# 35 pairs of projection blocks by seven half-size products, and the branch projections behind the mLSTM heads

## The chip, the cores and the metric
One core of a Trainium2 chip runs the kernel in one launch. The metric is device time in microseconds (us); the median of the runs is compared. The engines are PE (TensorE: matmuls, with PEld as its weight loads), DVE (VectorE), ACT (ScalarE), POOL (GpSimd) and SP (SyncE, which issues the transfers).

## The reference
One layer of a streaming encoder on 576 tokens (512 of a new stream, 64 of a running one), model width 1024:

```
h = rmsnorm(x);  p = h @ w_in                      # 1024 x 7880, columns split into 12 parts
hm = mlstm(conv(xcm), vm, i, f) * sigmoid(o)       # 4 heads of width 256, chunks of 64 tokens in the reference
ha = mla(c_q, c_kv, k_r)                           # 8 attention heads on latents
p_m = (hm * silu(z_m)) @ w_pm                      # 1024 x 1024
p_a = (ha * silu(z_a)) @ w_pa                      # 1024 x 1024
y = x + (sigmoid(g_m) * p_m + sigmoid(g_a) * p_a) @ w_out
```

States and caches of both streams are outputs too. Everything is float32.

## The kernel before
Each float32 operand is split in a high and a low part, and a product is three matmuls (hi hi, hi lo, lo hi). The inputs' parts (`hhi`, `hlo`) stay in SBUF with the features on partitions. A **block** is 128 output columns for all 576 tokens: `fblock` (L150) loads 512 KB of weights by `wload` (L107, two `raw` buffers), ACT writes the high part (128x1024, L104), DVE subtracts the low part (L105), and `gemm_f` (L120) issues 48 matmuls at L126: two halves of 288 tokens, three products, eight parts of the inner dimension, each half in its own PSUM bank (`MM`, two buffers).

There are 72 such blocks' worth of work: 8 each of z_a (Z), g_m (G) and g_a, 32 in the four mLSTM heads (conv input, o, z_m, v), 8 of w_pa and 8 of w_pm. With the heads' own q and k products that is 3,648 matmuls at L126.

The order: normalised input and latents (`START`); then the attention loop, which follows `PLAN`: K (keys and queries of a pair of heads, L567), H (a head, L524), Z (`z_block` L516), G (`gm_block` L170, its result goes to a DRAM scratch) and P (`proj_a` L584: a pair of heads times w_pa, added up in the SBUF tile `part`, L593 and L595). Then four mLSTM heads (`mhead` L685): `conv_block` (L638) x2, `gate_block` (L673) x2, `v_block` (L659) x2, q and k, and the loop over chunks (L730), where POOL makes the scaled queries (L752, split at L105) and a reciprocal root (L74). The g_a blocks (`ga_block` L614, L619) stand around the heads: one before, seven after. Then w_pm with the merge (L815 to L826), and w_out with the residual (L828 to L854). Weights are split as they arrive, on ACT and DVE, one or two blocks ahead.

A scheduler in the framework sets the order of each engine's instructions when the program is built, and it moves independent blocks between the steps of the attention and of the chunk loop. So the order that runs is the built one, not that of the text. The PSUM is split in pools of 2 banks (`pmm`), 3 (`psa`) and 3 (`psk`), L46 to L48.

Of the kernel before, what the change touches and what calls it, by code (L numbers as in the profile page):

```python
# [27 lines left out]
# order in which the work of the first two stages is issued (see `steps` and the attention loop)  # L28
START = "X0 A Q X1 C0 X2 B C1 S X3 X4 T0 L T1 T3 C3 C2 C4 T2 R T4 J"
PLAN = "G0 K0 Z0 H0 Z1 K1 H1 G2 G1 Z2 P0 H2 Z3 Z4 H3 G3 K2 P1 H4 G4 Z5 Z6 H5 G5 K3 Z7 P2 H6 H7 G6 G7 P3"  # L30
# [7 lines left out]
def layer(ctx: ExitStack, tc, A, O):  # L38
# [7 lines left out]
    pmm = mkpool(ctx, "pmm", 2, space=PSUM)  # L46
    psa = mkpool(ctx, "psa", 3, space=PSUM)
# [3 lines left out]
    wts = mkpool(ctx, "wts")  # L51
    hpool = mkpool(ctx, "hT")
    gp = mkpool(ctx, "gates")
    pp = mkpool(ctx, "part")

    def MM():
        return [pmm.tile([P, 512], F32, tag="mm", name="mm")[:, 0:HT] for _ in range(2)]
# [61 lines left out]

    def gemm_f(ps, w, x, nk, c0=0, k0=0):  # L120
        whi, wlo = w
        xhi, xlo = x
        trip = [(a, b, k) for a, b in ((whi, xhi), (whi, xlo), (wlo, xhi)) for k in range(nk)]
        for j, sl in enumerate(HALVES):
            for n, (a, b, k) in enumerate(trip):
                pe.matmul(ps[j], a[:, k0 + k, c0:c0 + P], b[:, k, sl], start=(n == 0), stop=(n == len(trip) - 1))  # L126
# [23 lines left out]
    def fblock(wd, col, x):  # L150
        w = wload([wd[:, col:col + P]], KB, P)
        ps = MM()
        gemm_f(ps, w, x, KB)
        return ps

    hx = (hhi, hlo)

# [10 lines left out]
    part = pp.tile([P, KB, T], F32, name="part")  # L168

    def gm_block(f, tg):  # L170
        z = fblock(A["w_in"], O_GM + f * P, hx)
        for j, sl in enumerate(HALVES):
            act.activation(tg[:, sl], z[j], AF.Tanh, scale=0.5)
        sp.dma_start(gmscr[f], tg)

    mla_es = ctx.enter_context(ExitStack())
    mp = mkpool(mla_es, "mla", side="right")
    cqhi = mp.tile([P, 3, T + DEC], F32R, name="cqhi")
# [3 lines left out]
    krhi = mp.tile([P, TK], F32R, name="krhi")  # L182
    krlo = mp.tile([P, TK], F32R, name="krlo")
# [4 lines left out]
    with ExitStack() as es:  # L188
        s0 = mkpool(es, "start0", side="right")
        s1 = mkpool(es, "start", side="right")  # L190
        sw = mkpool(es, "startw", side="right")
        s2 = mkpool(es, "start2", side="right")
# [13 lines left out]
        cgk = s2.tile([P, 5, ROPE], F32, name="cgk")  # L206
        sgk = s2.tile([P, 5, ROPE], F32, name="sgk")
        gq = s2.tile([P, ROPE], F32, name="gq")

        def load_small():  # L210
# [5 lines left out]
            for cg, sg, g in ((cgk, sgk, small["g_kr"]), (cgq, sgq, gq)):  # L216
# [34 lines left out]
        def x_tile(n):  # L251
            t0, L = TILES[n]
            xt = s1.tile([P, D], F32, tag="xt", name="xt", bufs=3)
# [4 lines left out]
            xs = s1.tile([P, D], F32, tag="xs", name="xs", bufs=1)  # L258
            act.activation(xs[0:L], xt[0:L], AF.Square, scale=D ** -0.5, accum_out=st[0:L, 0:1])
# [80 lines left out]
        def gates():  # L340
            # log-sigmoid, running sums and maxima; rows are (chunk, head)
# [77 lines left out]
        def load_q():  # L419
# [3 lines left out]
                 "T": ck_tile, "R": past, "J": gates,  # L423
                 "G": lambda f: gm_block(f, s1.tile([P, D], F32, tag="xt", name="tg", bufs=3)[:, 0:T])}
# [4 lines left out]
    with ExitStack() as es:  # L429
        hap = mkpool(es, "ha", side="right")  # L430
        cw = mkpool(es, "cw", side="right")
        ap = mkpool(es, "att", side="right")
        ak = mkpool(es, "atk", side="right")
        aq = mkpool(es, "atq", side="right")
# [81 lines left out]
        def z_block(h):  # L516
            z = fblock(A["w_in"], O_ZA + h * P, hx)
            za = aq.tile([P, T], F32, tag="za", name="za", bufs=2)
            for j, sl in enumerate(HALVES):
                act.activation(za[:, sl], z[j], AF.Tanh, scale=0.5)  # L520
                dve.scalar_tensor_tensor(za[:, sl], za[:, sl], 1.0, z[j], ALU.add, ALU.mult)
            return za

        def head(hh, qT, qrT, kT, v, za, ha):  # L524
# [29 lines left out]
            pTs = aq.tile([P, 2, DEC], F32, tag="pTs", name="pTs", bufs=1)  # L554
# [10 lines left out]
            split_of(ha[0][:, hh], ha[1][:, hh], za)  # L565

        def kq(p):  # L567
# [4 lines left out]
            wk = wload([A["w_ukv"][:, 512 * p:512 * (p + 1)]], 2, 512, cw, 6 * QH)  # L572
            wq = wload([A["w_uq"][:, 2 * QH * p:2 * QH * (p + 1)]], 3, 2 * QH, cw, 6 * QH)
# [10 lines left out]
        def proj_a(p, ha):  # L584
            for c in range(2):
# [38 lines left out]
    with ExitStack() as es:  # L624
# [60 lines left out]
        def mhead(h):  # L685
# [14 lines left out]
            for e in range(2):  # L700
                v_block(2 * h + e, va, e)
# [204 lines left out]
```

## Time and profile before

| | |
|---|---|
| median of 3 runs (lowest, highest) | 824.47 us (824.22, 824.84) |
| profiled execution, first to last instruction | 822.5 us |
| PE busy | 810.0 us, 98% |
| DVE busy | 478.7 us, 58% |
| ACT busy | 362.0 us, 44% |
| POOL busy | 141.4 us, 17% |
| HBM read, written | 64.24 MB, 7.61 MB |

The profiled execution has only its span, 822.5 us; the median of the runs is 2.0 us above it. Busy shares are means over stages: input and attention run up to about 368 us, the mLSTM heads and g_a to 714 us, w_pm to 765 us, and w_out to the end.

### The profile page before, as it was taken

What the parts mean: (1) busy time and instruction counts of PE and PEld (TensorE: products, weight loads), DVE (VectorE), ACT (ScalarE), POOL (GpSimd) and SP (SyncE); (2) the same over time, 40 slices, a digit from 0 to 9 for tenths busy, and PEclk for the clock granted to TensorE, in tenths of its full rate; (3) what the DMA queues carried; (4) which work ended last, traced back from release to release, by engine and by line L of the source; (5) the groups of instructions that cost most, each with busy time, mean ns of one, the idle gap of its engine ahead of it and who ended that gap; (6) DMA issues with size and microseconds to landing.
All of it is one profiled execution on the core that took longest, in us unless ns stands there. A gap on an engine that the chain in (4) does not pass through costs nothing.

```text
span 822.5 us, 14924 instructions
## 1 busy us (share of the span) xinstructions
PE 810.0 (98%) x5759; PEld 761.5 (93%) x5759; DVE 478.7 (58%) x1211; ACT 362.0 (44%) x999; POOL 141.4 (17%) x253
## 2 busy tenths in 40 slices
PE   7899999999999999999999999999999999999998
PEld 6898997888898798889999999999999999999997
DVE  5666566755576658545534873775477355655431
ACT  5446556663555654322434544444454434332200
POOL 2343241410143133001001110110111011000000
PEclk9999999999999999999999999999999999999999
DMA  8431231013113011126223232333333432543332
GB/s 267 138 108 59 74 111 27 1 52 106 41 52 120 27 41 33 46 84 157 78 77 91 66 106 74 103 84 97 91 94 96 118 87 68 165 124 106 101 95 76
DMA packets 101742, 72.80 MB, mean 89 GB/s; under 512 B 5742, under 2 KB 95848, under 8 KB 101672
## 3 DMA queue, kind: packets, MB, share of 16 engines
q1 hardware_dynamic: 101672, 71.86, 30.5%
q8 instruction: 45, 0.74, 0.4%
q14 instruction: 25, 0.20, 0.1%
HBM read 64.24 MB, written 7.61 MB: 87 GB/s over the span
## 4 chain that ended last, share of the span: by engine, by line
PE 94%; DMA 3%; DVE 1%; ACT 1%; issue 0%; SPq 0%; POOL 0%; DVEq 0%; ACTq 0%
PE mm L126 58%; PE sk L143 10%; PE sk L852 3%; PE sa L852 3%; PE sa L529 2%; PE sa L728 2%; PE sa L559 2%; PE sk L728 2%; PE sk L136 2%; PE sa L531 1%; PE sa L547 1%; PE sk L745 1%; PE sa L136 1%; PE sk L502 1%; DMA part<-in_w_in 1%; DMA E<-gscr 1%
## 5 line engine op out<-in xcount | busy, mean ns | idle before, releaser
L105 DVE TENSOR_TENSOR wlo<-raw,whi 128x1024 fp32r<-128x1024 f32 (+1 forms) x88 | 108.5, 1234 | 92.1 <-ACT whi L104 87.1
L104 ACT CAST whi<-raw 128x1024 fp32r<-128x1024 f32 (+1 forms) x88 | 92.6, 1055 | 135.2 <-PE mm L126 91.9
L126 PE MATMUL mm<-hhi,whi 128*128 128x288 f32 x896 | 147.1, 300 | 1.1 <-ACT hhi L104 1.1
L126 PE MATMUL mm<-hhi,wlo 128*128 128x288 f32 x896 | 146.6, 299 | 0.0
L126 PE MATMUL mm<-hlo,whi 128*128 128x288 f32 x896 | 145.7, 298 | 0.0
L126 PEld LDWEIGHTS mm<-hhi,whi 128*128 128x128 f32 x896 | 126.6, 188 | 2.1 <-ACT hhi L104 1.4
L126 PEld LDWEIGHTS mm<-hlo,whi 128*128 128x128 f32 x896 | 127.1, 188 | 1.3 <-issue 0.5
L126 PEld LDWEIGHTS mm<-hhi,wlo 128*128 128x128 f32 x896 | 126.9, 188 | 1.2 <-issue 0.5
L74 POOL TENSOR_TENSOR r<-r,mhalf 128x2 f32<-128x2 f32 (+3 forms) x44 | 37.2, 844 | 165.4 <-DVE r L495 109.4
L126 PE MATMUL mm<-ha,whi 128*128 128x288 f32 x256 | 48.2, 307 | 0.6 <-DVE part L595 0.6
L126 PEld LDWEIGHTS mm<-ha,whi 128*128 128x128 f32 x256 | 37.3, 188 | 2.7 <-DVE part L595 1.1
L511 ACT ACTIVATE P<-sa,sc 128x128 f32<-128x128 f32 (+4 forms) x40 | 20.1, 503 | 36.4 <-DVE sc L510 35.6
L752 POOL TENSOR_TENSOR qi<-qf,wi 128x256 f32<-128x256 f32 (+1 forms) x16 | 11.9, 744 | 105.7 <-ACT qf L710 54.3
L595 DVE TENSOR_TENSOR part<-part,mm 128x288 f32<-128x288 f32 x48 | 21.4, 452 | 11.8 <-PE mm L126 11.6
L74 POOL TENSOR_TENSOR sc<-sc,mhalf 128x1 f32<-128x1 f32 (+1 forms) x20 | 13.0, 648 | 87.0 <-DVE sc L784 87.0
L126 PE MATMUL mm<-ha,wlo 128*128 128x288 f32 x128 | 27.5, 296 | 0.0
L105 POOL TENSOR_TENSOR qi<-qi,qi 128x256 fp32r<-128x256 f32 (+1 forms) x16 | 10.7, 668 | 85.3 <-ACT qi L104 85.3
L529 PE MATMUL sa<-kT,qT 128*128 128x128 f32 (+3 forms) x64 | 23.4, 447 | 0.0
L510 DVE TENSOR_REDUCE sc<-sa 128x1 f32<-128x128 f32 (+4 forms) x40 | 18.3, 457 | 8.5 <-PE sa L532 6.4
L728 PE MATMUL sk<-va,kw 128*128 128x258 f32 (+1 forms) x120 | 22.2, 290 | 0.1
L823 DVE SCALAR_TENSOR_TENSOR mt<-tgm,mm 128x288 f32<-128x288 f32 x16 | 7.3, 454 | 25.1 <-PE mm L126 25.1
L474 ACT ACTIVATE qT<-sk,gqn_c 128x128 f32<-128x128 f32 (+1 forms) x40 | 12.2, 354 | 18.8 <-PE sk L472 18.8
(353 smaller groups left out, 1641.0 us busy)
## 6 DMA issues: line engine op xcount, KB each, us to landing
raw<-in_w_in SPq DMA_DIRECT2D x56, 512.0 KB, 3.8
raw<-in_w_pa SPq DMA_DIRECT2D x8, 512.0 KB
raw<-in_w_pm SPq DMA_DIRECT2D x8, 512.0 KB, 4.2
raw<-in_w_uq SPq DMA_DIRECT2D x4, 576.0 KB, 4.0
gmscr<-tg SPq DMA_DIRECT2D x8, 288.0 KB
tgm<-gmscr SPq DMA_DIRECT2D x8, 288.0 KB, 4.3
xt<-in_x_prompt SPq DMA_DIRECT2D x4, 512.0 KB, 6.7
raw<-in_w_ukv SPq DMA_DIRECT2D x4, 512.0 KB, 3.8
```

Of the source, the lines that this page charges most:

```text
L74: pool.tensor_tensor(dst, ms, mhalf[0:n, 0:dst.shape[-1]], op=ALU.pow)
L104: act.copy(hi, src)
L105: (eng or dve).tensor_tensor(lo, src, hi.bitcast(F32), op=ALU.subtract)
L126: pe.matmul(ps[j], a[:, k0 + k, c0:c0 + P], b[:, k, sl], start=(n == 0), stop=(n == len(trip) - 1))
L136: pe.matmul(out, x[:, k, t0:t0 + P], a, start=(i == 0), stop=(i == len(trip) - 1))
L143: pe.matmul(out, b[:, k, t0:t0 + L], a[:, k, c0:c0 + n], start=(i == 0), stop=(i == len(trip) - 1))
L510: dve.tensor_reduce(sc[0:L, 0:1], ps, AX.X, ALU.max, negate=True)
L511: act.activation(pt[0:L, 0:n], ps, AF.Exp, bias=sc[0:L, 0:1], accum_out=sc[0:L, 1:2])
L529: pe.matmul(ps[:, 0:n], qT[hh][:, q0:q0 + P], kT[hh][:, 0:n], start=True, stop=False)
L595: dve.tensor_tensor(part[:, f, sl], part[:, f, sl], ps[j], op=ALU.add)
L728: pe.matmul(out, x, y, start=(first and i == 0), stop=(last and i == 2))
L852: pe.matmul(ps[0:L, 0:NB], x[:, 4 * u + k, t0:t0 + L], w[u][i][:, k], start=(q == 0), stop=(q == len(trip) - 1))
```

## The change
Two neighbouring blocks with the two halves of the inner dimension and the two halves of the tokens form a 2x2 by 2x2 product of half-size matrices. `spair` computes it by seven products (Strassen in Winograd's form) instead of eight: 7 x 12 matmuls of 288 columns (three split products, four parts of the inner dimension) instead of 96. The seven weight matrices are four sub-blocks of `raw` and three sums, with a fourth sum for the last product; POOL makes four sums in place in `raw`, and each of the seven is split on its own. The inputs' sums T1 to T4 are made once per operand. The results are put together partly in a PSUM bank that several products add to, with ACT copies (three) and DVE adds (three) between.

35 pairs go this way: Z 4, g_m 3, heads 16, g_a 4, w_pa 4, w_pm 4. One g_m pair stays plain (`G0`). The program has 5,210 matmuls instead of 5,630. `ha`, `hm` and the gates of g_a go to DRAM scratch; w_pa is no longer part of the attention loop, it stands behind the heads, and the sums for `ha` and `hm` are made there (`operand`).

```diff
-PLAN = "G0 K0 Z0 H0 Z1 K1 H1 G2 G1 Z2 P0 H2 Z3 Z4 H3 G3 K2 P1 H4 G4 Z5 Z6 H5 G5 K3 Z7 P2 H6 H7 G6 G7 P3"
+PLAN = "K0 Z0 H0 K1 H1 Z1 M1 H2 H3 K2 Z2 M2 H4 H5 K3 Z3 M3 H6 H7"
+N_SA = 3
+RING = 5
-    pmm = mkpool(ctx, "pmm", 2, space=PSUM)
+    pst = mkpool(ctx, "pst", space=PSUM)
-    psk = mkpool(ctx, "psk", 3, space=PSUM)
+    psk = mkpool(ctx, "psk", 5 - N_SA, space=PSUM)
+    def combos(f11, f12, f21, f22, dst, eng):
+        eng.tensor_tensor(f11, f12, f11, op=ALU.subtract)
+        split_of(*dst[0], f11)
+        eng.tensor_tensor(f12, f22, f12, op=ALU.subtract)
+        eng.tensor_tensor(f22, f22, f11, op=ALU.subtract)
+        split_of(*dst[1], f22)
+        split_of(*dst[2], f12)
+        eng.tensor_tensor(f21, f21, f22, op=ALU.subtract)
+        split_of(*dst[3], f21)
+    def spair(wd, col, X, ct):
+        raw = rawp.tile([P, 2 * D], F32, tag="raw", name="raw", bufs=2).rearrange("p (k c) -> p k c", k=KB)
+        sp.dma_start(raw, wd[:, col:col + 2 * P].rearrange("(k p) c -> p k c", p=P))
+        f11, f12, f21, f22 = (raw[:, k:k + KH, c:c + P] for c in (0, P) for k in (0, KH))
...
+        a11 = sw(f11)
+        pool.tensor_tensor(f11, f11, f21, op=ALU.subtract)
+        pool.tensor_tensor(f21, f21, f22, op=ALU.add)
+        px, pz = bank(tx), bank(tz)
+        prod(px, a11, "B11", True)
+        act.copy(ct[:, 0, 0:HT], px)
+        s1 = sw(f21)
+        pool.tensor_tensor(f21, f22, f11, op=ALU.subtract)
+        prod(pz, s1, "T1", True)
+        act.copy(ct[:, 1, HT:T], pz)
+        s2 = sw(f21)
+        prod(px, s2, "T2", False)
+        act.copy(ct[:, 0, HT:T], px)
+        a12 = sw(f12)
+        pool.tensor_tensor(f12, f12, f21, op=ALU.subtract)
+        py = bank(ty)
+        prod(py, a12, "B21", True)
+        dve.tensor_tensor(ct[:, 0, 0:HT], ct[:, 0, 0:HT], py, op=ALU.add)
+        s3 = sw(f11, 1)
+        prod(px, s3, "T3", False)
+        dve.tensor_tensor(ct[:, 1, HT:T], ct[:, 1, HT:T], px, op=ALU.add)
+        s4 = sw(f12, 1)
+        prod(pz, s4, "B22", False)
+        dve.tensor_tensor(ct[:, 0, HT:T], ct[:, 0, HT:T], pz, op=ALU.add)
+        a22 = sw(f22, 1)
+        prod(px, a22, "T4", False)
+        return px
+    def gated(lp, tag, ct, scr, wd, q, p):
+        tg = lp.tile([P, 2, T], F32, tag=tag, name="tg", bufs=2)
+        sp.dma_start(tg, scr[2 * p:2 * p + 2].rearrange("f p t -> p f t"))
+        px = spair(wd, 2 * p * P, q, ct)
+        dve.scalar_tensor_tensor(tg[:, 0], tg[:, 0], 1.0, ct[:, 0], ALU.add, ALU.mult)
+        dve.scalar_tensor_tensor(tg[:, 1, HT:T], tg[:, 1, HT:T], 1.0, ct[:, 1, HT:T], ALU.add, ALU.mult)
+        dve.scalar_tensor_tensor(tg[:, 1, 0:HT], tg[:, 1, 0:HT], 1.0, px, ALU.add, ALU.mult)
+        return tg
...
         for h in range(H_M):
-            if h == 0:
-                ga_block(0, lp)
             mhead(h)
-        for f in range(1, KB):
-            ga_block(f, lp)
+        for p in range(KB // 2):
+            gate_out(PT(), O_GA, gascr, p)
...
+        operand(f1, "g", hascr, aq)
+        for p in range(KB // 2):
+            ct = PT()
+            ta = gated(lp, "gm", ct, gascr, A["w_pa"], aq, p)
+            sp.dma_start(gascr[2 * p:2 * p + 2].rearrange("f p t -> p f t"), ta)
+        operand(f1, "g", hmscr, hq)
...
+            tg = gated(lp, "gm", ct, gmscr, A["w_pm"], hq, p)
+            dve.tensor_tensor(tg, tg, ta, op=ALU.add)
+            split_of(mt[0][p], mt[1][p], tg)
```

`sw` gives a sub-block's high and low part a slot in a ring of five (`wh`, `wl`), from the heads on with three further slots for the last three of a pair; `operand` loads a branch's result from scratch and makes its 14 split parts, with `combos` on POOL (8 sums of 128x576).

On PE, in the w_pm stage, one block was three rows of 16 matmuls in two groups; the names are output bank, input part and weight part.

```order
L126 MATMUL mm<-hmhi,whi 128x288 x8
L126 MATMUL mm<-hmlo,whi 128x288 x8
L126 MATMUL mm<-hmhi,wlo 128x288 x8
L126 MATMUL mm<-hmhi,whi 128x288 x8
L126 MATMUL mm<-hmlo,whi 128x288 x8
L126 MATMUL mm<-hmhi,wlo 128x288 x8
```

Now, in the same stage, the products of two pairs stand between each other (banks b_9595 and b_9596 are of one pair, b_9735 and b_9736 of the next).

```order
L205 MATMUL b_9595<-hhi,wh_9664 128x288 x4
L205 MATMUL b_9595<-hlo,wh_9664 128x288 x4
L205 MATMUL b_9595<-hhi,wl_9665 128x288 x4
L205 MATMUL b_9735<-hhi,wh 128x288 x4
L205 MATMUL b_9735<-hlo,wh 128x288 x4
L205 MATMUL b_9735<-hhi,wl 128x288 x4
L205 MATMUL b_9736<-T1h,wh 128x288 x4
L205 MATMUL b_9736<-T1l,wh 128x288 x4
L205 MATMUL b_9736<-T1h,wl 128x288 x4
L205 MATMUL b_9595<-T4h,wh_9698 128x288 x4
L205 MATMUL b_9595<-T4l,wh_9698 128x288 x4
L205 MATMUL b_9595<-T4h,wl_9699 128x288 x4
```

So two products of the next pair (24 matmuls) stand between the last two products of a pair that add to one bank.

On POOL, in the chunk loop of a head, there were a scaled query, its split and a reciprocal root per chunk (`qi`, `sc`).

```order
L105 TENSOR_TENSOR qi_7323<-qi,qi_7322 128x256
L752 TENSOR_TENSOR qi<-qf,wi 128x256
L74 TENSOR_TENSOR sc<-sc,mhalf 128x1
L105 TENSOR_TENSOR qi_8236<-qi,qi_8235 128x256
L752 TENSOR_TENSOR qi<-qf,wi 128x256
L74 TENSOR_TENSOR sc<-sc,mhalf 128x1
```

Now the sums of the weights in `raw` stand between them (head 3, with g_a pairs beside it).

```order
L870 TENSOR_TENSOR qi<-qf,wi 128x256
L221 TENSOR_TENSOR raw<-raw 128x4x128
L208 TENSOR_TENSOR raw<-raw 128x4x128
L209 TENSOR_TENSOR raw<-raw 128x4x128
L214 TENSOR_TENSOR raw<-raw 128x4x128
L75 TENSOR_TENSOR sc<-sc,mhalf 128x1
L221 TENSOR_TENSOR raw<-raw 128x4x128
L106 TENSOR_TENSOR qi_8006<-qi,qi_8005 128x256
```

The root of a chunk stands behind up to four sums of 128x512.

On DVE, at the start of w_pm, each block had one split of 128x1024, two merges out of PSUM, an add and a split of the merged block.

```order
L823 SCALAR_TENSOR_TENSOR mt<-tgm,mm 128x288
L105 TENSOR_TENSOR hlo<-mt,hhi 128x576
L823 SCALAR_TENSOR_TENSOR mt<-tgm,mm 128x288
L105 TENSOR_TENSOR wlo<-raw,whi 128x1024
L824 TENSOR_TENSOR mt<-mt,part 128x576
```

Now, behind the heads, the splits of `ha` and its sums (`aB11l` to `aT4l`, from the tile `g`) stand in a row with weight splits and an add (L227).

```order
L106 TENSOR_TENSOR wl_8803<-raw,wh_8802 128x512
L227 TENSOR_TENSOR ct<-ct,b_8516 128x288
L106 TENSOR_TENSOR aB21l<-g,aB21h 128x576
L106 TENSOR_TENSOR aB22l<-g,aB22h 128x576
L106 TENSOR_TENSOR aT1l<-g,aT1h 128x576
L106 TENSOR_TENSOR aT3l<-g,aT3h 128x576
L106 TENSOR_TENSOR wl_8820<-raw,wh_8819 128x512
L106 TENSOR_TENSOR wl_8837<-raw,wh_8836 128x512
L106 TENSOR_TENSOR aT2l<-g,aT2h 128x576
L106 TENSOR_TENSOR aT4l<-g,aT4h 128x576
L106 TENSOR_TENSOR aB11l<-g,aB11h 128x576
```

Weight splits that PE needs next stand in the same queue as the splits of the operand.

## Rows read from the trace of the kernel before
**Rows 1.** The page, busy time of each engine (us, share of the span, instructions).

```profile
PE 810.0 (98%) x5759; PEld 761.5 (93%) x5759; DVE 478.7 (58%) x1211; ACT 362.0 (44%) x999; POOL 141.4 (17%) x253
```

**Rows 2.** Engine waits on PE, the two largest (total us, times, longest).

```profile
PE sa L267 <- DVE xs L262: 2.7, 2, 1.4
PE sk L203 <- DVE wrm L200: 1.5, 1, 1.5
```

**Rows 3.** Windows: length; PE, PEld, DVE, ACT, POOL busy; clock, DMA share, GB/s.

```profile
0.00:368.00 368.00, 359.99 (x2304) 317.78 (x2305) 231.27 (x665) 192.85 (x650) 97.12 (x181) 1.00 0.26 77
368.00:714.00 346.00, 345.44 (x2624) 339.45 (x2623) 203.68 (x477) 150.46 (x326) 39.96 (x56) 1.00 0.34 94
714.00:765.30 51.30, 51.30 (x389) 51.28 (x388) 26.02 (x38) 13.91 (x19) 3.31 (x14) 1.00 0.44 130
765.30:822.50 57.20, 53.22 (x449) 53.01 (x447) 17.71 (x32) 4.75 (x6) 1.03 (x2) 0.99 0.29 88
558.20:630.50 72.30, 72.30 (x553) 70.93 (x553) 45.45 (x113) 33.43 (x75) 9.88 (x14) 1.00 0.35 96
```

**Rows 4.** Chain of waits, the w_pm piece (start us, us, what).

```profile
714.33 50.97 PE mm L126 x384
```

**Rows 5.** Groups by shape, whole span (count | busy us, mean ns | idle before).

```profile
L105 DVE TENSOR_TENSOR ulo<-acc,uhi 128x512 fp32r<-128x512 f32 x8 | 5.5, 684 | 0.7 <-ACT uhi L104 0.7
L105 DVE TENSOR_TENSOR ha<-za,ha 128x576 fp32r<-128x576 f32 x8 | 6.1, 768 | 2.5 <-ACT ha L104 2.5
L105 DVE TENSOR_TENSOR hmlo<-tm,hmhi 128x1152 fp32r<-128x1152 f32 x4 | 5.4, 1356 | 1.7 <-ACT hmhi L104 1.7
L595 DVE TENSOR_TENSOR part<-part,mm 128x288 f32<-128x288 f32 x48 | 21.4, 452 | 11.8 <-PE mm L126 11.6
L104 ACT CAST uhi<-acc 128x512 fp32r<-128x512 f32 x8 | 5.0, 620 | 5.5 <-DVE acc L655 5.5
L593 ACT COPY part<-mm 128x288 f32<-128x288 f32 x16 | 6.4, 398 | 2.9 <-PE mm L126 2.8
L752 POOL TENSOR_TENSOR qi<-qf,wi 128x256 f32<-128x256 f32 x12 | 10.1, 839 | 0.9
L105 POOL TENSOR_TENSOR qi<-qi,qi 128x256 fp32r<-128x256 f32 x12 | 8.8, 737 | 83.4 <-ACT qi L104 83.4
```

**Rows 6.** Groups by shape, POOL and DVE in the head of 558.2 to 630.5 us.

```profile
L105 POOL TENSOR_TENSOR qi<-qi,qi 128x128 fp32r<-128x128 f32 x1 | 0.5, 460 | 0.5 <-ACT qi L104 0.5
L105 DVE TENSOR_TENSOR wlo<-raw,whi 128x1024 fp32r<-128x1024 f32 x9 | 11.0, 1223 | 14.5 <-ACT whi L104 13.4 <-ACT uhi L104 1.1
L652 DVE SCALAR_TENSOR_TENSOR acc<-xp,cols,acc 128x579 f32<-128x579 f32 x6 | 4.9, 815 | 0.0
L105 DVE TENSOR_TENSOR C<-Cf,C 128x516 fp32r<-128x516 f32 x4 | 3.2, 800 | 0.0
```

**Rows 7.** Timeline, POOL and DVE in chunk loops (start us, us, instruction).

```profile
520.08 1.09 DVE L773 SCALAR_TENSOR_TENSOR Cf<-Cf,decB,sk 128x258 f32<-128x258 f32 x2
520.58 0.73 POOL L105 TENSOR_TENSOR qi<-qi,qi 128x256 fp32r<-128x256 f32 x1 [10.11 <-ACT qi L104]
...
543.64 0.74 POOL L752 TENSOR_TENSOR qi<-qf,wi 128x256 f32<-128x256 f32 x1
...
543.78 1.15 DVE L105 TENSOR_TENSOR C<-Cf,C 128x516 fp32r<-128x516 f32 x1
```

**Rows 8.** Timeline, a POOL operation that started behind one of DVE's.

```profile
521.09 0.84 DVE L652 SCALAR_TENSOR_TENSOR acc<-xp,cols,acc 128x579 f32<-128x579 f32 x1
521.39 1.14 POOL L752 TENSOR_TENSOR qi<-qf,wi 128x256 f32<-128x256 f32 x1
521.85 0.20 DVE L781 TENSOR_SCALAR sc<-sa,emc 64x1 f32<-64x1 f32 x1
```

**Rows 9.** Page, the attention's softmax groups, DVE and ACT.

```profile
L511 ACT ACTIVATE P<-sa,sc 128x128 f32<-128x128 f32 (+4 forms) x40 | 20.1, 503 | 36.4 <-DVE sc L510 35.6
L510 DVE TENSOR_REDUCE sc<-sa 128x1 f32<-128x128 f32 (+4 forms) x40 | 18.3, 457 | 8.5 <-PE sa L532 6.4
```

More of the change, by code (lines that the diff above doesn't have):

```diff
@@ L148, in fold, with PT, bank, MM @@
         dve.tensor_tensor(dst, dst, ps[0:DEC], op=ALU.add)
[L150 to L154, printed above, removed]
-    hx = (hhi, hlo)
+    hx = (hhi, hlo)
+    ring2 = []
+    ring = ["b0", "b1", "b2"]
+    KH = KB // 2
+    def PT():
+        return ctp.tile([P, 2, T], F32, tag="ct", name="ct", bufs=2)
+    def bank(tag):
+        return pst.tile([P, 512], F32, tag=tag, name=tag)[:, 0:HT]
+    def MM():
+        out = []
+        for _ in range(2):
+            ring.append(ring.pop(0))
+            out.append(bank(ring[-1]))
+        return out
@@ new lines, in combos, with sw, prod @@
+    def combos(f11, f12, f21, f22, dst, eng):
[11 more added lines that the diff above has]
+        f11, f12, f21, f22 = (raw[:, k:k + KH, c:c + P] for c in (0, P) for k in (0, KH))
+        def sw(f, more=0):
+            if more and ring2:
+                w = [ring2[0].tile([P, KH, P], F32R, tag=t, name=t, bufs=3) for t in ("wh2", "wl2")]
+            else:
+                w = [wr.tile([P, KH, P], F32R, tag=t, name=t, bufs=RING) for t in ("wh", "wl")]
+            split_of(*w, f)
+            return w
+        tx, tz, ty = ring
+        ring[:] = [ty, tz, tx]
+        def prod(ps, a, b, first):
+            trip = [(p, q, k) for p, q in ((0, 0), (0, 1), (1, 0)) for k in range(KH)]
+            for n, (p, q, k) in enumerate(trip):
+                pe.matmul(ps, a[p][:, k], X[b][q][:, k], start=(first and n == 0), stop=(n == len(trip) - 1), skip_group_check=True)
+        a11 = sw(f11)
[25 more added lines that the diff above has]
+        return px
@@ L582, in kq @@
             return qT, qrT, kT, v
-        def proj_a(p, ha):
-            for c in range(2):
-                w = wload([A["w_pa"][2 * P * p:2 * P * (p + 1), 512 * c:512 * (c + 1)]], 2, 512)
-                for e in range(4):
-                    f = 4 * c + e
-                    ps = MM()
-                    gemm_f(ps, w, ha, 2, c0=e * P)
-                    for j, sl in enumerate(HALVES):
-                        if p == 0:
-                            act.copy(part[:, f, sl], ps[j])
-                        else:
-                            dve.tensor_tensor(part[:, f, sl], part[:, f, sl], ps[j], op=ALU.add)
-        tens, zas, has = {}, {}, {}
+        tens, zas = {}, {}
         for tok in PLAN.split():
@@ L601, in layer @@
                 tens[i] = kq(i)
[L602 to L603 removed]
+            elif kind == "M":
+                gate_out(PT(), O_GM, gmscr, i)
+            elif kind == "A":
+                gate_out(PT(), O_GA, gascr, i)
             elif kind == "Z":
[L605 to L609 removed]
+                zas[i] = z_pair(i)
             else:
[L611 removed]
+                head(i, i % 2, *tens[i // 2], zas[i // 2][:, i % 2])
     mla_es.close()
[L614 to L619 removed]
+    ring2.append(mkpool(ctx, "ring2"))
     NP = 3 + T + 3
```

323 lines of the change are left out of this document (176 added, 147 removed).

## The prediction
> **What bounds the kernel now.** I read the busy times of the page first: PE is busy 810.0 of 822.5 us, no other engine above 58% [rows 1]. Then the waits on PE, because a full share could hide short stalls: the largest releaser costs it 2.7 us in the whole span [rows 2]. Then the windows, because the share is a mean: PE has 360.0 of 368.0 us in input and attention, 345.4 of 346.0 in heads and g_a, all of the w_pm stage, and 53.2 of 57.2 in w_out, at the full clock (1.00, the 2.4 GHz level) everywhere [rows 3]. So the kernel lasts as long as its matmuls do, and the other engines have room. How much room decides this case, so I read the same rows for DVE and POOL: in one head DVE is busy 45.45 of 72.30 us and POOL 9.88 [rows 3].
>
> **What is removed.** The w_pm stage is nothing but matmuls of the kind that go: 384 in 50.97 us, 0.1327 us each [rows 4]. 35 pairs drop 12 each, 420 in all, which is the fall of the matmul count from 5,630 to 5,210. 420 x 0.1327 = 55.7 us. While PE sets the end, the span goes from 822.5 to 766.8 us; with the 2.0 us by which the median of the runs stands above the profiled span, 768.8 us. By stages, in matmuls: w_pa's 384 (51.0 us) leave the attention, which also loses 7 x 12 (11.1 us): 368 - 62.1 = 306 us. Heads and g_a lose 20 x 12 (31.8 us): 314 us. w_pa and w_pm are 8 pairs of 84, 11.15 us each: 89.2 us. w_out stays at 57.2 us.
>
> **What is added, per pair.** DVE: seven splits of 128x512 at 0.684 us for two of 128x1024, and three adds of 128x288 out of PSUM at 0.452 us [rows 5]: 6.1 us. ACT: seven casts at 0.620 and three copies at 0.398 us: 5.5 us. POOL: four sums of 128x512, which no row shows. The same kind takes 0.460 us at 128 columns [rows 6] and 0.737 at 256 [rows 5], so 2.16 ns a column on a fixed 0.18 us: 1.29 us. The lower bound is the 256-column time, 0.74 us; the upper one goes from 0.460 to the other 256-column row, 0.839 us: 1.60 us. I take 1.29, since the 0.839 row holds waits (below): 5.2 us a pair. Each is far under the pair's 11.15 us on PE, and every one is hidden if the three engines work side by side.
>
> **They don't quite.** In the timeline POOL's product started at 543.64 and ended at 544.38; a DVE split (two inputs in SBUF) started at 543.78, took 1.15 us where ones of its size take 0.68, and ended at 544.93, 0.55 us after POOL [rows 7]. By the rows of 512 and 1152 columns DVE costs 1.05 ns a column on a fixed 0.15 us [rows 5], so 0.54 us is the data time of 516 columns: it began its data when POOL was done. The other way round, POOL's product started at 521.39 under a DVE operation that ended at 521.93 and took 1.14 us, ending 0.60 us after it, again its data time [rows 8]. Against that, two DVE operations with one input in PSUM took 1.09 us for the pair across a POOL split that kept its 0.73 us [rows 7]. So I read: a DVE operation with two SBUF inputs and a POOL tensor operation exclude each other for their data time; PSUM inputs do not.
>
> The Trainium skill (SBUF - State Buffer, section Who interferes with whom) says the same: DVE's second SBUF input comes through an interface shared with GpSimd, and the later instruction blocks fully until the first is done. The rows agree (1.15 against 0.68 us). It adds that issue order decides who blocks, which speaks against this change, for whatever is queued behind the blocked instruction waits too; that is the second rival below.
>
> The Trainium skill (GPSIMD Engine Reference, section 4.1 Engine selection) puts two-input elementwise work on GpSimd at about twice VectorE's time. By it a 128x512 sum would be an estimated 1.37 us, and the four 5.5 us; no run here shows one.
>
> **The sum of the exclusive time.** Data times: DVE 0.54 us for 512 columns, 0.61 for 576, 1.21 for 1152; POOL 1.11 for 512, 1.25 for 576. A pair: 7 x 0.54 + 4 x 1.11 = 8.2 us, under 11.15. A w_pa pair has two merges from SBUF more (576 and 288 columns, 0.9 us): 9.1. A w_pm pair has the add and split of 1152 columns besides: 11.5, over 11.15. Each operand (`ha`, `hm`) is 14 splits of 576 and 8 POOL sums: 18.5 us with no matmul of its own. Last stage: 4 x 9.1 + 4 x 11.5 + 18.5 = 101 us against PE's 89, **+12**. The other operand stands on POOL and DVE beside the four g_a pairs, which have 4 x 8.2 = 33 us of their own and 44.6 us of PE: 51 against 44.6, **+7**.
>
> **The heads.** Per head PE goes from 72.3 to 65.9 us. DVE starts from 45.45, where overlapping ends count once: consecutive operations overlap by 0.08 us (the one from 521.09 to 521.93 and that at 521.85) [rows 8]. Nine splits go (11.0 us, some 10.4 net) [rows 6] and that of `hm` (1.3); 28 splits of 0.61 net, two for q and k and 12 adds of 0.38 come: 56.8 us. POOL goes to 9.9 + 16 x 1.29 = 30.5 us. Both still fit. But DVE works in order: when a split waits for POOL, the adds out of PSUM, the chunk's state (`C`) and the merge of its output stand behind it, and PE waits for these; the root in each chunk (L74 before) now stands behind up to four sums on POOL. What share s of POOL's time falls on DVE's queue no row tells: between 0 (POOL runs under PSUM operations and idle DVE) and 1. At s = 0.3 the queue is 65.9 us, as long as PE's. More than half of DVE's time in a head is for operations with two SBUF inputs (the splits, `acc`, `C`) [rows 6], so I take more, 0.4: 56.8 + 12.2 = 69.0 us, 3.1 over PE, four heads **+12**.
>
> **Input and attention**: seven pairs and the sums of the input on POOL, DVE at 231 of 368 before and PE at 306 now, one PSUM bank less for the attention (`psk` 2), and no w_pa blocks to fill its gaps: **+4**, between 0 and the third rival's price. Inside a pair the product that adds to a bank after an ACT copy or DVE add has 12 to 24 other matmuls (1.6 to 3.2 us) between, against 0.40 or 0.45 us for the copy: nothing. The transfers grow by the scratch of `ha`, `hm` and the gates; w_pm ran at 0.44 of the DMA engines with 512 KB loads [rows 3], and a pair takes as many weight bytes in 11.15 us as two blocks in 12.7: nothing.
>
> Sum: 822.5 - 55.7 + 12 + 7 + 12 + 4 = 801.8, with the 2.0 us outside the span **804 us**.
>
> **Rivals.** (1) PE stays the bound: s under 0.3 in the heads, and w_pm's splits spread over the stage. For it: three engines at most at 86% of a pair's PE time; PE almost never waited before. Against: the last stage's 101 and 51 us are sums of times that exclude each other. 769 us, up to 780 with part of the last stage.
>
> (2) The other side: DVE's queue takes POOL's time nearly whole. Place: heads and the last stage. At s = 0.7 a head is 56.8 + 21.4 = 78.2 us, 12.3 over PE, four +49; in the last stage DVE has 72 us (56 splits and 24 adds net, merges, 14 operand splits) and POOL 8 x 5.2 + 11.4 = 53, together 109, +20; g_a with its operand 32 + 0.7 x 32 = 54 against 44.6, +10; with +4, 768.8 + 83 = 852 us. It decides from about s = 0.55: heads +31, last stage and g_a +20, attention +4 make 55, all of the gain. For it: in order queues, sums in rows of three or four on POOL, each as long as two splits. Against: POOL's operation ran beside PSUM operations at no cost to either [rows 7], and weights are split ahead in five to eight slots.
>
> (3) The attention pays: w_pa's 51 us of matmuls no longer fill it. A softmax row needs DVE's maximum (0.457 us) and ACT's exponential (0.503) in turn, 40 times [rows 9]: 38 us if every one shows, 19 if half do, in place of the 4: 804 + 15 = 819 us. For it: ACT already waited 35.6 us for these maxima [rows 9]. Against: PE bridged all of them, and Z and g_m pairs are still there.
>
> That the change does not do what it says falls out: the count of matmuls is in the program.
>
> **How the numbers follow.** Forecast (788 to 816) 0.47, rival 1 0.16, rival 3 0.13, rival 2 0.24. Rivals 1 and 3 are faster with the forecast, save a tail of 3; a measurement here tells 0.2%, 1.65 us, from no change. Faster 0.73, same 0.04, slower 0.23. The range 774 to 838 leaves out half of rival 1 and the upper half of rival 2.
>
> **What would show it.** PE's matmuls of 288 columns fewer by 420 at 0.133 us, and its idle time up by about 35 us, most of it behind DVE's weight splits, in the heads and after them; POOL's 128x512 sums at 1.2 to 1.7 us; DVE's 128x512 splits longer than 0.684 us in the mean (0.8 to 1.1), its adds out of PSUM still near 0.45. Wrong it would be with PE idle under 10 us (rival 1), with PE waiting mostly for ACT, POOL or a DMA, or with the attention's window well over 310 us.

## The result: slower by 7.7%, and the profile after

The changed kernel takes 888.03 us (median of 4 runs, 885.76 to 889.99) against 824.59 us on the same chip: ratio 1.077, interval 1.0752 to 1.0789. The forecast was 804 us, the range 774 to 838. The loss is 63.4 us where a gain of 20 was forecast: a miss of 84 us.

First the engines' totals in the trace after (us, share of the span, instructions), which answer to [rows 1].

```profile
PE 787.5 (89%) x5339; PEld 717.2 (81%) x5339; DVE 699.9 (79%) x1469; ACT 459.6 (52%) x1274; POOL 420.2 (48%) x433
```

The 420 matmuls are gone (5,759 to 5,339), but PE is busy only 22.5 us less where 55.7 were to go, and stands idle for 96 of 883.7 us. DVE went from 478.7 to 699.9 us. Then the stages after (columns as in [rows 3]): all of input and attention, two stretches of it, heads and g_a, w_pa and w_pm, w_out.

```profile
0.00:369.10 369.10, 325.62 (x1930) 273.77 (x1931) 270.10 (x687) 204.34 (x699) 182.92 (x249) 0.96 0.24 75
71.00:135.20 64.20, 44.74 (x214) 36.55 (x214) 53.99 (x121) 32.46 (x111) 52.10 (x62) 0.76 0.20 62
135.20:369.10 233.90, 217.85 (x1281) 177.57 (x1281) 178.80 (x482) 138.70 (x512) 107.17 (x139) 1.00 0.18 59
369.10:697.60 328.50, 304.35 (x2245) 291.40 (x2246) 288.90 (x602) 184.34 (x447) 162.45 (x133) 0.99 0.33 103
697.60:820.80 123.20, 98.32 (x659) 93.10 (x659) 110.46 (x129) 59.24 (x110) 69.76 (x46) 0.93 0.56 185
820.80:883.70 62.90, 59.20 (x510) 58.89 (x508) 30.44 (x53) 11.63 (x20) 5.05 (x5) 0.99 0.38 120
```

| stage | before [rows 3] | forecast | after | matmuls, forecast and after |
|---|---|---|---|---|
| input and attention | 368 | 306 + 4 | 369.1 | 1,836, 1,930 |
| heads, g_a | 346 | 314 + 12, g_a + 7 | 328.5 | 2,384, 2,245 |
| w_pa, w_pm (before: w_pm) | 51.3 | 89 + 12 | 123.2 | 672, 659 |
| w_out | 57.2 | 57.2 | 62.9 | 449, 510 |

The attention lost 374 matmuls (2,304 to 1,930), 49.6 us at 0.1327, and is as long as before: 59 us over the forecast. The last two rows hold 28 us more. The heads' 328.5 us look as forecast, but the windows do not hold the matmuls that the forecast had in them: the built order runs 94 more in the first, 139 fewer in the heads', and 61 more in that of w_out. With these counted at 0.1327 us each, the attention is 47 us over the forecast, the heads 14, w_pa and w_pm 24, and w_out 2 under. The reader is to see in the second window (71 to 135 us) that DVE and POOL are busy more than 80% of it each, PE 70%, and that the granted clock is 0.76 there: PE, kept waiting, spent part of that stretch at the lower level of 1.2 GHz. Over the whole span it was at that level for 52.6 us (before: 1.3), with 128 matmuls started in it; those of 288 columns start 0.24 us apart there in place of 0.133. So up to some 14 us of the loss (an estimate, 128 x 0.107) came by way of the clock, behind the waits; no run parts the two.

Next the groups by shape that answer to [rows 5] (count | busy, mean ns | idle before).

```profile
L106 DVE TENSOR_TENSOR wl<-raw,wh 128x512 fp32r<-128x512 f32 x273 | 227.3, 850 | 35.5 <-ACT wh L105 32.1
L224 DVE TENSOR_TENSOR ct<-ct,b 128x288 f32<-128x288 f32 x35 | 15.6, 444 | 4.3 <-PE b L205 2.9 <-ACT ct L212 1.1 <-issue 0.2
L208 POOL TENSOR_TENSOR raw<-raw 128x512 f32<-128x512 f32 x35 | 52.7, 1506 | 59.3 <-DVE wl L106 56.8
```

The sizes were well bounded: a sum takes 1.45 us in the mean of its four lines (the row shown is the slowest, 1.51; taken: 1.29, at most 1.60), undisturbed 1.28; an add out of PSUM 0.444. A split takes 0.850 instead of 0.684 us.

PE's waits name something else than the forecast did (total us, times, longest).

```profile
PE b L205 <- DVE ct L227: 10.1, 8, 2.4
PE b L205 <- DVE ct L224: 5.4, 6, 1.4
PE b L205 <- DVE wl L106: 5.0, 5, 1.3
```

All waits for a pair's adds and copies (`ct`) together are 29.1 us, 21.8 of them on DVE; those for weight splits are 5.0.

### The profile page after: what moved, and what is told of

It is laid out like the page before. It is cut to its first block, busy times and chain, and to the rows that moved or that the text cites. A ratio compares the mean times of both kernels' runs of the same rounds, so it can differ in the third digit from the quotient of the medians.

```text
span 883.7 us, 14917 instructions
## 1 busy us (share of the span) xinstructions
PE 787.5 (89%) x5339; PEld 717.2 (81%) x5339; DVE 699.9 (79%) x1469; ACT 459.6 (52%) x1274; POOL 420.2 (48%) x433
## 4 chain that ended last, share of the span: by engine, by line
DVE 38%; PE 36%; DMA 10%; POOL 6%; issue 6%; ACT 4%; SPq 1%; DVEq 0%; ACTq 0%; POOLq 0%
DVE wl L106 12%; PE b L205 11%; PE sk L145 7%; DMA raw<-in_w_in 4%; PE sa L977 2%; PE sk L977 2%; PE b L128 2%; DMA E<-gscr 2%; DVE acc L774 2%; PE sa L697 2%; PE sa L667 1%; ACT wh L105 1%; DVE hlo L106 1%; DVE ct L227 1%; DVE ct L230 1%
## 5 line engine op out<-in xcount | busy, mean ns | idle before, releaser
L106 DVE TENSOR_TENSOR wl<-raw,wh 128x512 fp32r<-128x512 f32 x273 | 227.3, 850 | 35.5 <-ACT wh L105 32.1
L105 ACT CAST wh<-raw 128x512 fp32r<-128x512 f32 x273 | 160.7, 618 | 148.3 <-DMA raw<-in_w_in 29.0
L205 PE MATMUL b<-hhi,wh 128*128 128x288 f32 x496 | 91.2, 303 | 13.6 <-DVE ct L224 5.4
L205 PE MATMUL b<-hhi,wl 128*128 128x288 f32 x496 | 91.2, 300 | 2.4 <-DVE wl L106 2.4
L205 PE MATMUL b<-hlo,wh 128*128 128x288 f32 x496 | 89.0, 297 | 0.0
L205 PEld LDWEIGHTS b<-hhi,wh 128*128 128x128 f32 x496 | 72.3, 189 | 18.0 <-DVE ct L224 6.7
L208 POOL TENSOR_TENSOR raw<-raw 128x512 f32<-128x512 f32 x35 | 52.7, 1506 | 59.3 <-DVE wl L106 56.8
L221 POOL TENSOR_TENSOR raw<-raw 128x512 f32<-128x512 f32 x35 | 51.6, 1475 | 60.1 <-DVE wl L106 49.0
L205 PEld LDWEIGHTS b<-hhi,wl 128*128 128x128 f32 x496 | 73.8, 188 | 4.5 <-DVE wl L106 3.1
L205 PEld LDWEIGHTS b<-hlo,wh 128*128 128x128 f32 x496 | 73.6, 189 | 0.1
L214 POOL TENSOR_TENSOR raw<-raw 128x512 f32<-128x512 f32 x35 | 48.1, 1374 | 51.6 <-DVE wl L106 48.5
L209 POOL TENSOR_TENSOR raw<-raw 128x512 f32<-128x512 f32 x35 | 51.2, 1464 | 1.9
L647 ACT ACTIVATE P<-sa,sc 128x128 f32<-128x128 f32 (+4 forms) x40 | 20.1, 503 | 28.5 <-DVE sc L646 27.6
L75 POOL TENSOR_TENSOR sc<-sc,mhalf 128x1 f32<-128x1 f32 (+1 forms) x20 | 17.3, 866 | 28.9 <-DVE sc L902 28.3
L205 PE MATMUL b<-T2h,wh 128*128 128x288 f32 x124 | 24.3, 311 | 2.6 <-ACT ct L212 2.6
L592 DVE TENSOR_SCALAR qs<-qs,r 128x64 f32<-128x64 f32 (+1 forms) x40 | 15.0, 375 | 12.9 <-POOL r L75 12.9
```

The lines of the kernel that those rows point to most:

```text
L75: pool.tensor_tensor(dst, ms, mhalf[0:n, 0:dst.shape[-1]], op=ALU.pow)
L105: act.copy(hi, src)
L106: (eng or dve).tensor_tensor(lo, src, hi.bitcast(F32), op=ALU.subtract)
L205: pe.matmul(ps, a[p][:, k], X[b][q][:, k], start=(first and n == 0), stop=(n == len(trip) - 1), skip_group_check=True)
L208: pool.tensor_tensor(f11, f11, f21, op=ALU.subtract)
L209: pool.tensor_tensor(f21, f21, f22, op=ALU.add)
```

## The experiments

The theories. S: the sums on GpSimd, and what they block, are the loss. M: the new order is, since w_pa's matmuls filled the attention's gaps for nothing. Each median is compared with the kernel before on the same chip (824.2 to 824.8 us).

**1. Eight products everywhere, new order kept (e1_plain).** Each pair makes four splits and four outputs of 24 matmuls; no sum is left.

```diff
+            for c, j, tag in ((0, 0, tx), (0, 1, tz), (1, 1, ty), (1, 0, tx)):
...
+                ps = bank(tag)
+                trip = [(u, p, q, k) for u in range(2) for p, q in ((0, 0), (0, 1), (1, 0)) for k in range(KH)]
...
+                if (c, j) != (1, 0):
+                    act.copy(ct[:, c, HALVES[j]], ps)
```

> All 35 pairs computed by eight products (four splits, 96 matmuls, no sums of weights, inputs or branches), everything else of the changed kernel kept: the order with w_pa behind the heads, the scratch, the PSUM pools. PE's work is that of the kernel before. Theory S (the sums that GpSimd makes, and what they block, are the loss): PE stays busy and the time is near the kernel before, 820 to 835 us, the stretch up to the first head of the mLSTM about 320 us. Theory M (the move is the loss: the attention without w_pa's 51 us of matmuls is a chain of short waits): 850 to 875 us, that stretch 345 us or more and the loss all in it. Theory C (both by halves): 835 to 850 us.

867.52 us, ratio 1.0513 (1.0495 to 1.0532). With the matmuls of the kernel before, the order, with the fetch of the branches, costs 43 us: S alone falls. The attention, from the first head's scores to the last head's output, first in the kernel before, then in this one (columns as in [rows 3]):

```profile
104.10:357.00 252.90, 252.90 (x1579) 217.36 (x1578) 161.56 (x475) 132.89 (x483) 62.34 (x110) 1.00 0.19 56
```

```profile
118.20:352.50 234.30, 226.98 (x1331) 186.61 (x1331) 143.95 (x444) 127.75 (x488) 61.67 (x111) 0.99 0.17 56
```

248 matmuls fewer made it 18.6 us shorter, 0.075 us each; in a row one of 288 columns costs 0.1327 [rows 4]. PE looks busy in both, but a matmul that stands alone counts its whole 0.3 us (the mean of the 288-column matmuls on the page of the kernel before is 300 ns). The busy share hid the room that w_pa was filling. How much room there was, the mean of 0.160 us a matmul (252.9 by 1,579) does not tell, since the kinds differ: from start to start, in a row, those of 384 and 512 columns take 0.17 and 0.23 us, and the unsplit float32 ones of scores and outputs up to 0.43. With each kind at its own spacing, the stretch before holds some 233 us of matmuls and this one 201 (estimates from the start times in the two traces): 20 and 34 us were room. So w_pa's matmuls were in part free there, not for nothing.

**2. Seven products in heads and g_a only (e2_heads)**, Z, g_m, w_pa and w_pm plain, the input's sums late in the attention.

> Seven products only in the heads and g_a (20 pairs); Z, g_m, w_pa and w_pm pairs by eight, without the branches' sums; the input's sums are made late in the attention instead of ahead of it. Theory S: attention 320 us, heads and g_a 330 as in the changed kernel, the last two stages at PE's 102 and 55: 800 to 812 us, faster than the kernel before. Theory M: the attention still takes 345 us or more, so 830 to 845 us.

864.62 us, ratio 1.0475 (1.0448 to 1.0503): hardly better than plain, above both expectations. In its trace the attention ends 12 us later than in the plain kernel (364.4 against 352.4 us), with the input's sums in it, and from there to w_pa's first matmul it takes 329 us against 346. So the 20 pairs saved 16 us, of 31.8 by the count, and the input's sums took most of it back.

**3. No sums of weights (e3_no_wsum).** The four `pool.tensor_tensor` lines of a pair are taken out.

> The changed kernel without the four GpSimd sums of the weights in each pair (the products are made with the four sub-blocks as they are, some twice; all splits, matmuls, copies and adds stay; what is left out is the sums' arithmetic). Theory S with the shared lock: 140 sums of some 1.4 us go, the splits of 128x512 fall from 0.85 to 0.69 us, heads from 328 to about 315 us, the last stage from 132 to 105, the attention by 10 to 15: 825 to 840 us. Theory M: only the heads and the last stage gain, the attention nothing: 845 to 860 us. If the sums don't matter: 880 or more.

832.79 us, ratio 1.0099 (1.0084 to 1.0114): 55.2 us for the 140 sums, as S had it. The heads fall from 328.5 to 303.7 us, the splits to 0.738 us; the attention ends 12 us earlier, at 357.0, where M had nothing. M alone falls too. Its heads, and its w_pa and w_pm:

```profile
357.00:660.70 303.70, 296.81 (x2240) 289.95 (x2240) 243.06 (x604) 187.42 (x448) 45.87 (x58) 0.99 0.36 111
660.70:765.00 104.30, 90.00 (x629) 86.96 (x628) 87.64 (x124) 57.06 (x107) 27.32 (x18) 0.95 0.64 211
```

**4. No sums of the input (e4_no_insum).**

> The changed kernel without the 32 GpSimd sums of the input ahead of the attention (the three operand sums are filled by splits of plain input parts; what is left out is the sums' arithmetic). Theory S: PE's idle time of some 25 us between 71 and 135 us goes, with it the low clock there: 850 to 860 us. Theory M: the idle time is moved, not removed: 875 us or more.

881.1 us (1.0665 to 1.0715): 6.9 us, not the idle time in that stretch, which is 19.5 us by the row above (64.20 less 44.74; the expectation's 25 was too much). It was mostly moved, as M said: the first scores start 11 us earlier (124.2 against 135.2 us), the attention ends 5 us earlier.

**5. A memset in the place of each sum (e5_memset), 6. three memsets (e14_memset3).** One of the four places, with one memset:

```diff
-        pool.tensor_tensor(f11, f11, f21, op=ALU.subtract)
+        pool.memset(f11, 0.0)
```

> The changed kernel with each of the four GpSimd sums of a pair replaced by a GpSimd memset of the same part of the weights (same place in the order, same waits before and behind it; it writes and reads nothing from SBUF; what is left out is the sums' arithmetic). Theory P (DVE's second SBUF input and GpSimd's reads exclude each other): DVE's splits of 128x512 fall from 0.85 to about 0.69 us and the time to 830 to 845 us, as without the sums (832.8). Theory L (the sums' place in the chain of load, split, sum, split is the loss, whatever GpSimd does there): 865 us or more, with the splits at 0.69 all the same.

> The changed kernel with three GpSimd memsets of the same part in the place of each sum of weights: about 1.6 us in that place, as long as a sum, the same waits, no reads of SBUF (what is left out is the sums' arithmetic). Theory P (the shared port): as with one memset, 835 to 850 us, DVE's splits at 0.70 to 0.73 us. Theory L (the time in the chain): back towards the changed kernel, 870 us or more, with splits at 0.70 to 0.73 us all the same. Half and half: 855 to 865.

One memset: 843.76 us (1.0189 to 1.0257), inside P's range; three: 853.96 (1.0336 to 1.0397), between P's range and that of half and half. The first three rows are from the second run, the last from the changed kernel.

```profile
L106 DVE TENSOR_TENSOR wl<-raw,wh 128x512 fp32r<-128x512 f32 x273 | 189.7, 711 | 45.5 <-ACT wh L105 39.0 <-PE b L205 2.8 <-PE sa L138 1.7
L208 POOL MEMSET raw<- 128x512 f32 x35 | 18.6, 530 | 7.9 <-DVE wl L106 7.9
L211 POOL MEMSET raw<- 128x512 f32 x35 | 18.5, 528 | 60.8 <-DMA raw<-in_w_in 40.2 <-DVE ct L232 8.0 <-DMA raw<-in_w_pa 7.2
L209 POOL TENSOR_TENSOR raw<-raw 128x512 f32<-128x512 f32 x35 | 51.2, 1464 | 1.9
```

Three take 1.6 us, somewhat longer than a sum, and the splits stay at 0.711 us. The waits around them are not quite the same, against the expectation: a memset reads nothing, so the ones on `f21` (L211) wait for the load, where the sum in that place (L209) ran right behind the one of L208, which waits for a split. So of the sums' 55.2 us, 21.2 (853.96 - 832.79) are what GpSimd's time costs in that shorter chain of load, split, sum, split; the other 34.1 go with a sum's reads, with DVE's longer operations and with the order among the sums, which these runs do not part. Both theories were half right.

**7. All four sums on DVE (e9_dve_sums), 8. two and two (e11_half_sums).**

```diff
-        pool.tensor_tensor(f11, f11, f21, op=ALU.subtract)
+        dve.tensor_tensor(f11, f11, f21, op=ALU.subtract)
```

> The changed kernel with the four sums of each pair on DVE instead of GpSimd. Theory P: no GpSimd sum waits for DVE or makes it wait, but DVE has 4 x 0.69 us more a pair; in the heads that is 56.8 + 9.8 = 67 us against PE's 66: 850 to 875 us. Theory L: the sums come in DVE's own order without a hand-over, 835 to 850 us.

> The changed kernel with two of the four sums of a pair on DVE and two on GpSimd. If the exclusive time of the shared port is what counts (a pair holds it 8.2 us with all four on GpSimd, 7.1 with two, 5.9 with none): between the changed kernel's 888 and the 871 with all on DVE, 876 to 884 us. If the length of the two queues counts (each gets shorter than in either of the two): 855 to 868 us.

870.95 us (1.0545 to 1.0592) and 886.52 (1.073 to 1.0767). All on DVE is 17 us better than all on GpSimd, though DVE carries four times 25 us more; the time lies in theory P's range (850 to 875), far above L's (835 to 850). Halving gains next to nothing, and neither reading fits it. Its trace shows a hand-over that the other two lack, GpSimd's second sum waiting for DVE's first:

```profile
L209 POOL TENSOR_TENSOR raw<-raw 128x512 f32<-128x512 f32 x35 | 56.2, 1607 | 125.1 <-DVE raw L208 116.1 <-DVE r L631 6.2 <-DVE r L588 1.5
```

That this is what eats the gain was not tested.

**9. Three PSUM banks for the attention's products: in the plain kernel, taken from the projections (e6_plain_psk3), and in the changed one, from the scores (e13_psk3).**

> The kernel with all pairs by eight products and the new order (867.5 us), but two PSUM banks for the projections and three instead of two for the attention's products. Theory M (the attention's own chain sets its length, 350 us with or without w_pa's matmuls, which were free there): the stretch up to the first mLSTM head stays at 345 to 355 us, 858 to 872 us in all. Theory B (the bank taken from the attention is the loss): that stretch falls towards PE's 300 us, 815 to 835 us in all.

> The changed kernel with the five attention and head banks split two and three instead of three and two. If the products' banks are short in the attention: 878 to 884 us, the attention shorter by 5 to 10 us. If the scores' banks are: 890 us or more. If neither: 886 to 889 us.

861.04 us (1.043 to 1.0465) against 867.52, and 891.42 (1.0755 to 1.0853) against 888.03. The bank is worth 6.5 us in the plain kernel, not the loss (its attention ends 16 us earlier, at 336.3 us, but most of that does not reach the end); in the changed one nothing beyond the spread of the runs.

**10. w_pa back in the attention (e8_wpa_back)**, with seven products in heads 1 to 3 and g_a only, w_pm plain.

> w_pa goes back into the attention loop (plain, added up in SBUF as before, then kept in scratch), Z, g_m, the first mLSTM head and w_pm by eight products, seven products in heads 1 to 3 and g_a (16 pairs); the input's sums are made during head 0. Theory M: the attention takes w_pa's 51 us for nothing and ends at 355 to 370 us; heads and g_a 335 to 345, w_pm 58 to 65, w_out 55: 805 to 830 us, near or below the kernel before. Theory B (the new layout, banks and buffers, slows the attention whatever is in it): the attention ends at 400 us or later, 850 us or more.

861.5 us (1.0423 to 1.046), worse than M expected. Its attention, with the share of w_pa's matmuls that ran up to its end (line L746; columns PE and PEld alone):

```profile
116.40:372.40 256.00, 252.04 (x1550) 213.84 (x1548) 164.10 (x491) 140.01 (x513) 65.25 (x110) 1.00 0.17 58
```

```profile
0.00:372.40 372.40, 45.80 (x291) 40.02 (x291) 1.00 0.25 79
```

With 291 matmuls of w_pa in it, the window up to there holds only 218 more than the plain kernel's (2,244 against 2,026), since other blocks moved behind it. These are 28.9 us at 0.1327, and input and attention are 19.9 us longer (372.4 against 352.5). So about a third of them was free there, not all. The gain was lost again in the heads (365.6 us, with the rest of w_pa and the input's sums), where 16 pairs of seven products stand.

**11. Without the step `operand`: changed kernel (e10_no_operand), plain kernel (e15_plain_no_operand).** With the fetch of the branches go their splits and, in the changed kernel, their 16 sums.

```diff
-        operand(f1, "g", hascr, aq)
...
-            ta = gated(lp, "gm", ct, gascr, A["w_pa"], aq, p)
+            ta = gated(lp, "gm", ct, gascr, A["w_pa"], hq, p)
...
-        operand(f1, "g", hmscr, hq)
```

> The changed kernel without the step that fetches ha and hm from scratch and makes their 28 split parts and 16 GpSimd sums; w_pa's and w_pm's pairs take the input's parts instead (what is left out: the branches' values). Theory O (PE stands at the start of w_pa and of w_pm for these operands): the last stage falls from 123 to about 100 us, 862 to 872 us in all. Theory W (the weights' sums bind that stage, the operands lie beside them): 120 us stays, 882 us or more.

> All pairs by eight products in the new order (867.5 us), and w_pa and w_pm take the input's parts instead of the branches fetched from scratch (what is left out: the branches' values). If the two long waits at the start of w_pa and w_pm (8.0 and 5.8 us in that run's trace) are what the fetch costs: 850 to 855 us, the rest (25 to 30 us over the kernel before) lies in the attention and the heads. If the attention is the whole of it: 862 us or more.

856.69 us (1.0361 to 1.041), 31.3 less than the changed kernel (below theory O's 862 to 872), and 853.05 (1.0319 to 1.0364), 14.5 less than the plain one. The stage of w_pa and w_pm in the first, without the step, weights' sums still in it:

```profile
700.00:791.20 91.20, 88.27 (x654) 86.56 (x653) 73.42 (x100) 42.41 (x83) 46.88 (x33) 1.00 0.64 216
```

91.2 us, with PE busy 88.3: without the step the weights' sums are all but hidden in that stage. With it they were not (that stage took 104.3 us in e3_no_wsum, 123.2 after): the operand's sums and the weights' stand in one queue on GpSimd. What of the 31.3 us is the fetch and what the step's splits and sums, these runs do not part. The trace of the changed kernel shows SP's queue there (start us, us; a long row is an issue that waits).

```profile
711.16 0.37 SPq L188 DMA_DIRECT2D raw<-in_w_pa  x1
712.50 0.36 SPq L258 DMA_DIRECT2D g<-hascr  x1
725.36 18.37 SPq L258 DMA_DIRECT2D g<-hmscr  x3
745.14 0.37 SPq L188 DMA_DIRECT2D raw<-in_w_pa  x1
746.11 0.36 SPq L945 DMA_DIRECT2D pascr<-tg  x1
750.47 0.36 SPq L258 DMA_DIRECT2D g<-hmscr  x1
```

The tile `g` has two buffers; a fetch waits until DVE and GpSimd have used up the one before. Three fetches of `hm` take 18.4 us to issue, and the weights of the next w_pa pair stand behind them: 34 us (711.16 to 745.14) without a weight load. That this gap held PE up is not shown: PE waits 2.4 us for weight splits in that stage. Its waits name the first operand at their head (total us, times, longest).

```profile
PE b L205 <- ACT aB11h L105: 7.2, 1, 7.2
PE b L205 <- DVE ct L227: 5.7, 4, 2.0
```

Of the 24.9 us that PE is idle there, 11.4 are waits for the operand's parts and 10.5 for adds out of PSUM.

**12. No sums and no step `operand` (e12_none).**

> The changed kernel without any sum (weights, input, branches) and without the branches' operands: seven products, their splits, copies and adds, the new order and scratch stores are all that is left (the sums' arithmetic and the branches' values are left out). If the causes add up: 832.8 without the weights' sums, less 7 for the input's and 17 to 25 for the operands: 800 to 810 us, so that the seven products alone are worth some 40 of their 55.7 us against the plain kernel in this order. If the waits move elsewhere: 815 to 830 us.

806.1 us, ratio 0.9785 (0.9741 to 0.9829), as the sum of causes had it. Its attention, its heads, and its w_pa and w_pm, which run at PE's full rate (82.7 us, all busy):

```profile
119.70:349.30 229.60, 216.50 (x1246) 174.85 (x1246) 155.81 (x479) 134.84 (x506) 73.97 (x112) 0.99 0.18 59
349.30:656.00 306.70, 298.50 (x2252) 291.65 (x2252) 241.40 (x603) 186.94 (x447) 42.83 (x56) 0.99 0.35 107
656.00:738.70 82.70, 82.70 (x628) 82.70 (x627) 58.17 (x99) 41.80 (x80) 3.16 (x4) 1.00 0.66 223
```

## Why the prediction was wrong, point by point

From the medians the loss adds up: 824.6, + 28.5 for the order in attention and heads (e15_plain_no_operand), - 47.0 for the seven products alone (806.1 against 853.05), + 81.9 for all sums and the step `operand` (888.0 against 806.1). Taken out one by one, weights' sums, that step and input's sums are 55.2, 31.3 and 6.9 us, 11.5 more than together: part of the loss needs two of them at once and goes when either is taken out.

- **The gain, 55.7 us.** The mechanism was right, the size 47.0: in the attention fewer matmuls do not shorten it one for one (with 96 fewer, 12.7 us, it ends at 349.2 us in e12_none and 351.5 in e15_plain_no_operand).
- **"Input and attention +4"** is the step that failed most, 59 us, of which 12 are the 94 matmuls more. What it sized too small are the order's room (e1_plain: 352.5 us, where the 278 matmuls fewer than before should have left 331) and sums (349.3 us without any, 369.1 with). The third rival named the mechanism, but its price, 38 us at most, came from the softmax alone, and the 32 sums of the input, some 26 us of GpSimd by the rows' own line, got no price of their own. The mistake is in the reading of [rows 2 and 3]: no wait on PE and a busy share of 98% were taken as a bound by matmuls alone, though some 20 of the 252.9 us were not. The forecast also took all of w_pa's 384 matmuls out of the window up to 368 us; 33 of them ran behind it.
- **The heads, +12 and g_a +7.** 328.5 us against 326 to 333 is luck: the window holds 139 matmuls, 18.4 us, fewer than the forecast had in it, so what was added to PE's time is 33 us and not 19. Without the weights' sums the heads take 303.7 us for five matmuls fewer.
- **"Inside a pair ... nothing."** The copies and adds between a pair's products were put at nothing, since 12 to 24 other matmuls stand between. In the trace after, PE waits 29.1 us for them, more than for anything else, and 5.0 for the weight splits that were to be most of its idle time. Without the weights' sums these waits are 13.5 us (e3_no_wsum), so it is in good part behind the sums that adds and copies come late.
- **The last stage, +12, with w_out 28 us off.** The 659 matmuls of w_pa and w_pm are 87 us and took 123.2, so 36 us and not 12 were added. Without the weights' sums the stage is 104.3 us, without the step `operand` 91.2, without both 82.7. The prediction priced the operand as work on DVE and POOL beside the pairs; PE stood 11.4 us for its parts. It did not ask what the fetch is queued behind, or what stands behind it on SP; how much that adds is not shown.
- **"PSUM inputs do not, two SBUF inputs do."** True but not whole. The timeline after shows one-input operations held as well (start us, us):

```profile
194.40 1.28 POOL L209 TENSOR_TENSOR raw<-raw 128x512 f32<-128x512 f32 x1
194.46 1.27 DVE L592 TENSOR_SCALAR qs<-qs,r 128x64 f32<-128x64 f32 x1 [1.13 <-POOL r L75]
...
195.84 0.24 DVE L592 TENSOR_SCALAR qs<-qs,r 128x64 f32<-128x64 f32 x1
```

The scaling of 128x64 (0.24 us alone) took 1.27 us and ended 0.05 us after GpSimd's sum. It is no single case: in that trace all 4 of these 32 that start under a weights' sum end with it (median 1.28 us, the others 0.25), and so do all 8 of the 16 casts of 128x128 at L602 that do (median 1.23 us, the others 0.23), while the 25 adds out of PSUM that start under one keep their 0.44. The attention is full of such operations, in chains of four engines, so a sum there delays more than a split; how much that is was not measured. The Trainium skill (SBUF - State Buffer, section Who interferes with whom) says that copies, casts and tensor_scalar can take the shared ports too, in their fast modes; the prediction used only the sentence on two inputs. These rows agree with it.
- **The rivals.** The second put its slower side in the heads and the last stage; the time was slower, in these two by 14 and 24 us over the forecast, but in the attention by 47. What decided was the third rival together with the sums and the operands. The prediction's own sign of being wrong came, the attention's window at 369 us where it had 310; PE's idle time rose by 84 us and not 35.

What stays open: in the heads of the plain kernel without the step `operand` a matmul takes 0.1361 us (330.5 by 2,428, trace of e15_plain_no_operand) against 0.1319 before [rows 3], some 10 us of the order's 28.5; which wait that is was not tried. Of the 34.1 us in experiments 5 and 6, the runs part neither the splits from the one-input operations nor these from the order among the sums.

No version here that computes the layer beats the kernel before. Even free of all sums and of the step `operand` the change would be worth 2.2% (1.7 to 2.6%), and the sums with that step cost over four times that.

## What to carry to other kernels

Where PE is never idle, still hold a stage's length against what its matmuls take in a row, each kind at its own spacing: if the stage is longer, it has a chain of its own, and work taken out of it can give back only part (here 18.6 us for some 33), while it costs in full where it is put. An operation that seems small on an idle engine is to be priced by its place in a chain and by the ports that it shares, and a fetch by what stands behind it in its queue.

## What had not been expected of the hardware

A sum of 128x512 on GpSimd takes 1.28 us undisturbed and a memset of that size 0.53. A DVE operation with one SBUF input (128x64, 0.24 us) took 1.27 us, held by GpSimd's sum until that ended; all 4 such scalings (L592) and all 8 casts (L602) that started under a sum ended within 0.09 us of it. The granted clock fell to 0.76 in a stretch of 64 us in which PE was busy 70%.
